# One division per head, a new order of units, and fewer first splits on VectorE in a hybrid encoder layer

## The chip, the cores and the metric

The kernel runs on one core of a Trainium2 chip. The metric is device microseconds of one execution, the median of several runs. TensorE (PE) does matrix products into PSUM, with its weight loads (PEld) beside them; VectorE (DVE) and ScalarE (ACT) do elementwise work on SBUF and PSUM; GpSimd (POOL) does elementwise work on SBUF; all transfers are issued from SyncE's queue (SP). TensorE's clock has two levels, 1.2 and 2.4 GHz; the profile gives the granted clock of a stretch as a share of the full one.

## The reference, cut to what matters

One layer over 2048 rows of 1024 columns, all in float32:

```python
h = rms_norm(x, norm_g)
proj = h @ w_in                       # 14 parts: a_q a_k a_v a_z m_q m_k m_v m_o m_z m_i m_f c_a c_b c_z
# A: band attention of 4 heads of 64 columns, 64-row chunks, 8 chunks back; gate silu(a_z)
# B: mLSTM of 4 heads of 128 columns:
num = s @ v + inter_w * (C @ q)       # s = (q k^T) * decay matrix
den = sum(s) + inter_w * (n . q)
h_ = num / max(|den|, exp(-m_t))
hm = rms_norm(sigmoid(m_o) * h_) * ml_out_g * silu(m_z)
# C: GLU of c_a, c_b; causal depthwise convolution of 31 taps; LayerNorm; silu; gate silu(c_z)
x = x + concat(A, B, C) @ w_out
```

## The kernel before, in words

The 2048 rows are worked off in four quarters (NQ) of 512, each of four blocks (NB) of 128. The work of a quarter is a list of *units*, each one projection: kv, qg (attention's q and the mLSTM gates, 264 columns), v and o (mLSTM) have rows on the partitions and go block by block (`tm`, lines 490 to 509); cb/ca (GLU), mk/mq/z (mLSTM k, q and gate of each head), az/cz (gates) and out0 to out7 (128 output columns each) have columns on the partitions and all 512 rows at once (`cm`, line 511). Each product is three passes: x and weights are each split into a rounded fp32r part and the rest, so one 128x512 result takes 3x8 = 24 matmuls.

The order of the units is written out by hand: FIRST for the first quarter, LATER + TAIL (lines 43 to 45) for the others. A quarter's eight outputs are the first units of the next list, mixed into it, and those of the last quarter stand alone at the end. Everything else (norms, attention, the mLSTM heads, convolutions) is written as generators, *chains*, that a planner in Python steps while it writes out the units' matmuls: it keeps a clock for every engine, with costs for each operation (lines 262 to 270), and puts a chain's next instructions into the program when their inputs should be ready by that clock. The order on each engine is fixed by that; on the chip only semaphores hold.

Weights come in pieces of 512 (qg: 528) columns through a ring of WB = 10 buffers. The first time, a piece is loaded raw (256 KB, four slots "W"), then split: a rounding copy and a subtraction. For the first eight pieces (kv's) the copies alternate between ACT and DVE and the subtractions between DVE and POOL; after that it is ACT and POOL (lines 450 and 451). The split piece is written to memory (512 KB) and later quarters load it from there. The first x is loaded in row blocks, its squares summed half on ACT and half on DVE (lines 556 to 561), the root taken on POOL, and then scaled and transposed on TensorE (`x_block`). x of later quarters arrives in transposed pieces k = 0 to 7 (`x_next`); only the first cb0 waits for them piece by piece (`xks`), and the outputs for the pieces of mT, the mixed result.

An mLSTM head (`head_chain`, line 963) multiplies, for each block, decayed scores and state into one PSUM tile, `ph`, of 129 columns: 128 numerators and, from a column of ones in vt, the denominator. DVE then updates the state `cst`, makes the reciprocal `rd` of the stabilised denominator in three [128x1] operations, and multiplies numerator, `rd` and the output gate `og` into `og` (lines 1019 to 1027). ACT sums the squares of each block. At the head's end POOL takes the root, ACT scales four blocks, TensorE transposes them (`pto`), and with the gate z they become a piece of mT. The 31-tap convolution runs as 60 DVE operations a quarter, `taps`, which the planner strews into DVE's free time; LayerNorm (`ln_chain`) is started behind mq3 and waits for the last tap. The last output unit is finished by one addition of 128x512 and one transfer.

Of the kernel before, what the change touches and what calls it, by code (L numbers as in the profile page):

```python
# [63 lines left out]
def kernel(ctx: ExitStack, tc: tile.TileContext, x, xT, wp, wq, norm_g, qg, kg, bias, far,  # L64
# [46 lines left out]
    def f(ap):  # L111
        return ap.bitcast(F32)
# [133 lines left out]
    class Engine:  # L246
# [3 lines left out]
        def __getattr__(self, name):  # L250
            fn = getattr(self.eng, name)

            def call(*a, **k):
# [174 lines left out]
    def feeder():  # L428
        while st["next"] < len(seq):
# [57 lines left out]

    PASS = ((0, 0), (0, 1), (1, 0))

    def tm(xt, u, b):  # L490
# [3 lines left out]
        step_ = 2 if gated else 1  # L494
        j0 = st["used"]
# [3 lines left out]
        for k in range(KT):  # L499
            w = piece((st["used"] if b == NB - 1 else j0 + k // step_))  # L500
            w = w[:, :, (k % step_) * n:(k % step_ + 1) * n] if gated else w
            need(xt[:, :, k, c])
# [8 lines left out]
    def cm(xt, u, ks=None):  # L511

        next_unit(u)
        ps = ps_new(u)
        i = 0
# [21 lines left out]
    def x_first(xt):  # L537
# [3 lines left out]
        big = io.tile([P, 2, D], F32, name="xbig", tag="og", bufs=1, cut=D)  # L541
# [8 lines left out]
        for b in range(NB):  # L550
# [4 lines left out]
            dump = ps_s.tile([P, D], F32, name="pdump", tag="s")  # L555
            A.activation(out=dump[:, 0:512], in_=t[:, 0:512], func=AF.Square, scale=1.0 / 32,
# [34 lines left out]
    def x_stat(q, rs, heads):  # L591
# [5 lines left out]
        big = io.tile([P, 2, D], F32, name="xbig", tag="og", bufs=1, cut=D)  # L597
# [243 lines left out]
    def gates(q, gt, FR, dd, cols, dec):  # L841
# [26 lines left out]
        R2_ = yield from take("R2", 256)  # L868
# [42 lines left out]
        shut(pt_)  # L911
        R2 = R2_[0:NR, :].rearrange("p (a b) -> p a b", a=2)
# [21 lines left out]
    def do_o(q, xt):  # L934
        next_unit("o")
        og = io.tile([P, NB, 512], F32, name="og", tag="og", bufs=1, cut=P)
        for b in range(NB):
            ps = tm(xt, "o", b)
            A.activation(out=og[:, b, :], in_=ps, func=AF.Tanh, scale=0.5)
            ps_done(ps)  # L940
            spawn(plus_one(og[:, b, :]))
        return og
# [20 lines left out]
    def head_chain(q, h, hb, vt, gc, cols, dec, FR, before):  # L963
# [43 lines left out]
        hs = slice(h * P, (h + 1) * P)  # L1007
        for b in range(NB):
# [25 lines left out]
        yield (rs,)  # L1034
        for b in range(NB):
            A.activation(out=og[:, b, hs], in_=og[:, b, hs], func=AF.Copy, scale=rs[:, b:b + 1])
# [3 lines left out]
        yield (og[:, :, hs],)  # L1040
        yield from bank_wait()
        pt, pt_ = bank("pto")
        for b in range(NB):
            tp(pt[:, b, :], og[:, b, hs])
# [18 lines left out]
    def do_conv(q, xt, j, ks=None):  # L1063
        pb = cm(xt, f"cb{j}", ks)
# [259 lines left out]
```

## Time and profile before

| | |
|---|---|
| median of 3 runs | 1214.1 us (1213.89 to 1214.77) |
| profiled execution | 1211.88 us, its span 1210.1 us, mean granted clock 0.993 |
| TensorE | 1172.0 us busy, 97% of the span |
| VectorE | 794.8 us, 66% |
| ScalarE | 432.7 us, 36% |
| GpSimd | 248.7 us, 21% |
| transfers | 240.25 MB, 199 GB/s on average |

The busy time of TensorE is modelled from pipelined matmuls; where it is busy throughout, the time of a group of 24 matmuls says how fast it goes. Idle time of an engine that is not the bottleneck costs nothing, so the shares are to be read stretch by stretch: the first quarter ends at about 282 us, and the last eight outputs begin at about 1161 us.

### The profile page before, as it was taken

To read this page: it belongs to the slowest core of one execution; us is meant where nothing else is said; L and a number is where in the kernel's file an instruction comes from. 1 tells how busy PE (TensorE), PEld (TensorE's weight loads), DVE (VectorE), ACT (ScalarE), POOL (GpSimd) and SP (SyncE) were. 2 spreads that over 40 slices of the span, in tenths; PEclk is the share of its full clock that TensorE was granted. 3 is DMA by queue.
4 is the path that set the end of the run, shared out by engine and by line. 5 is a ranking of instruction groups with operands and counts; after the bars stand their busy time and mean duration, and the time that the engine had idled before them with its cause. 6 is when DMAs were issued, how large, how long until landed. Compare 5 with 4: busy or idle time off the path is not lost.

```text
span 1210.1 us, 17636 instructions
## 1 busy us (share of the span) xinstructions
PE 1172.0 (97%) x6308; PEld 968.1 (80%) x6308; DVE 794.8 (66%) x1845; ACT 432.7 (36%) x984; POOL 248.7 (21%) x325
## 2 busy tenths in 40 slices
PE   6998998999999999999999999999999999999998
PEld 5776777777778888888888888888887988888886
DVE  6287888985568576775556766677447666677631
ACT  4454634443324441333232443233412344123310
POOL 5572545550232010111021100001002200011100
PEclk9998999998999999999999999999999999999999
DMA  9574848756774335654856351764684506375472
GB/s 356 167 302 158 305 153 300 263 209 205 270 260 143 114 132 199 238 173 155 298 197 232 123 175 53 278 200 143 213 292 160 205 27 213 131 251 164 157 230 101
DMA packets 95408, 240.25 MB, mean 199 GB/s; under 512 B 11288, under 2 KB 28248, under 8 KB 95320
## 3 DMA queue, kind: packets, MB, share of 16 engines
q1 hardware_dynamic: 95320, 239.11, 57.0%
q8 instruction: 50, 0.82, 0.3%
q14 instruction: 38, 0.31, 0.1%
HBM read 186.52 MB, written 52.56 MB: 198 GB/s over the span
## 4 chain that ended last, share of the span: by engine, by line
PE 83%; DVE 6%; DMA 4%; POOL 3%; issue 3%; ACT 1%; SPq 0%; POOLq 0%; ACTq 0%; DVEq 0%
PE pmm_out L311 13%; PE pmm_v L311 7%; PE pmm_z L311 7%; PE pmm_mk L311 7%; PE pmm_mq L311 6%; PE pmm_kv L311 6%; PE pmm_o L311 6%; PE pmm_cz L311 4%; PE pp L311 3%; PE pmm_qg L311 3%; PE po L311 3%; PE pmm_ca L311 3%; PE pss L311 3%; PE pmm_az L311 3%; PE ptp L316 3%
## 5 line engine op out<-in xcount | busy, mean ns | idle before, releaser
L254 DVE SCALAR_TENSOR_TENSOR cvu<-cvu,cvw_t 128x512 f32<-128x512 f32 x240 | 193.3, 806 | 10.9 <-ACT cvu L254 7.1
L311 PE MATMUL pmm_out<-mT,w 128*128 128x512 f32 x768 | 189.5, 398 | 2.8 <-DVE xr L254 1.7
L311 PEld LDWEIGHTS pmm_out<-mT,w 128*128 128x128 f32 x768 | 141.8, 188 | 34.7 <-DVE mT L254 2.5
L254 POOL TENSOR_TENSOR w<-rw,w 128x512 fp32r<-128x512 f32 (+1 forms) x80 | 114.3, 1443 | 175.6 <-ACT w L254 158.4
L311 PE MATMUL pmm_v<-w,xT 128*128 128x512 f32 x384 | 115.2, 417 | 1.2 <-POOL w L254 1.2
L311 PE MATMUL pmm_mk<-xT,w 128*128 128x512 f32 x384 | 106.2, 406 | 0.0
L311 PE MATMUL pmm_z<-xT,w 128*128 128x512 f32 x384 | 101.0, 409 | 0.0
L311 PE MATMUL pmm_mq<-xT,w 128*128 128x512 f32 x384 | 96.2, 397 | 0.0
L311 PE MATMUL pmm_o<-w,xT 128*128 128x512 f32 x384 | 95.4, 399 | 0.0
L311 PE MATMUL pmm_kv<-w,xT 128*128 128x512 f32 x384 | 94.2, 400 | 0.0
L311 PEld LDWEIGHTS pmm_kv<-w,xT 128*128 128x128 f32 x384 | 72.0, 190 | 16.0
L254 DVE SCALAR_TENSOR_TENSOR macc<-mraw,mcw_t,macc 128x512 f32<-128x512 f32 x96 | 79.4, 827 | 7.5 <-ACT macc L254 5.1
L311 PEld LDWEIGHTS pmm_z<-xT,w 128*128 128x128 f32 x384 | 72.4, 194 | 14.9
L311 PEld LDWEIGHTS pmm_o<-w,xT 128*128 128x128 f32 x384 | 71.0, 188 | 16.1 <-issue 0.9
L311 PEld LDWEIGHTS pmm_mq<-xT,w 128*128 128x128 f32 x384 | 71.0, 188 | 15.1 <-issue 0.5
L311 PEld LDWEIGHTS pmm_v<-w,xT 128*128 128x128 f32 x384 | 68.3, 191 | 15.0 <-POOL w L254 2.8
L311 PEld LDWEIGHTS pmm_mk<-xT,w 128*128 128x128 f32 x384 | 69.1, 189 | 13.2 <-issue 1.0
L254 POOL COPY mch<-mraw 128x3 f32<-128x3 f32 x32 | 11.0, 342 | 277.3 <-ACT mraw L254 276.9
L254 ACT CAST w<-rw 128x512 fp32r<-128x512 f32 (+1 forms) x80 | 49.1, 618 | 22.8 <-DMA rw<-in_wp 7.0
L254 ACT COPY pT<-ptp 128x384 f32<-128x384 f32 (+2 forms) x64 | 29.3, 459 | 77.7 <-PE ptp L316 77.6
L254 DVE TENSOR_TENSOR xr<-pmm_out,xr 128x512 f32<-128x512 f32 x32 | 22.0, 688 | 45.5 <-PE pmm_out L311 43.0
L311 PE MATMUL pmm_az<-xT,w 128*128 128x512 f32 x192 | 49.7, 401 | 0.0
(231 smaller groups left out, 1996.7 us busy)
## 6 DMA issues: line engine op xcount, KB each, us to landing
w<-wk SPq DMA_DIRECT2D x240, 512.0 KB, 4.4
wk<-w SPq DMA_DIRECT2D x80, 512.0 KB, 5.6
rw<-in_wp SPq DMA_DIRECT2D x80, 256.0 KB, 4.3
xr<-in_xT SPq DMA_DIRECT2D x32, 256.0 KB, 5.3
out<-xr SPq DMA_DIRECT2D x32, 256.0 KB, 5.3
xbig<-in_x SPq DMA_DIRECT2D x14, 512.0 KB, 6.9
w<-wk SPq DMA_DIRECT2D x12, 528.0 KB, 7.6
xk<-in_xT SPq DMA_DIRECT2D x24, 256.0 KB, 5.7
```

What stands on the lines that cost most here:

```text
L254: i = tc.keep_in_program_order(fn(*a, **k))
L311: tc.keep_in_program_order(PE.matmul(out_, lhsT=lhsT, rhs=rhs, start=start, stop=stop))
L316: tc.keep_in_program_order(PE.transpose(out=out_, in_=in_, identity=(ident_r if rnd else ident)[0:n, 0:n]))
```

## The change

- **Denominators.** `og` gets a 129th column a head, set to 1. The product from PSUM is taken 129 wide into it, so the denominator lands beside the gated numerators, undivided. After the fourth block `divide` makes the reciprocals of all four at once, ACT sums the squares with the reciprocal as scale, and the reciprocal is multiplied into the root before the head is scaled.
- **Order.** New lists FIRST, LATER and TAIL. `tm` too now waits for x piece by piece, by a table `filled`, since kv becomes the first unit that reads a later quarter's x.
- **First splits.** Of the first eight pieces DVE keeps the copy of piece 1 and the subtractions of pieces 0 and 3. The squares of the first x's blocks 1 to 3 are summed on ACT alone.
- **Last output.** The last unit is computed in two halves of 256 columns, each with its own addition and transfer.
- **Planner.** Other costs for POOL; the buffer R2 of the gates is taken later and from another set of slots.

```diff
-FIRST = ['kv', 'cb0', 'ca0', 'cb1', 'ca1', 'qg', 'v', 'mk0', 'mq0', 'o', 'mk1', 'mq1', 'az0', 'z0', 'mk2', 'mq2', 'az1', 'z1', 'mk3', 'mq3', 'cz0', 'cz1', 'z2', 'z3']
-LATER = ['out0', 'out1', 'out2', 'out3', 'cb0', 'ca0', 'kv', 'out4', 'cb1', 'ca1', 'qg', 'out5', 'v', 'mk0', 'mq0', 'o', 'out6', 'mk1', 'mq1', 'out7']
-TAIL = ['mk2', 'mq2', 'z0', 'mk3', 'mq3', 'z1', 'az0', 'az1', 'z2', 'cz0', 'cz1', 'z3']
+FIRST = ['kv', 'cb0', 'ca0', 'qg', 'cb1', 'ca1', 'v', 'mk0', 'mq0', 'o', 'mk1', 'mq1', 'az0', 'z0', 'mk2', 'mq2', 'cz0', 'mk3', 'mq3', 'az1', 'cz1', 'z1', 'z2', 'z3']
+LATER = ['out0', 'out1', 'out2', 'out3', 'kv', 'cb0', 'ca0', 'cb1', 'ca1', 'qg', 'v', 'out4', 'out5', 'out6', 'mk0', 'mq0', 'out7', 'o', 'mk1', 'mq1']
+TAIL = ['mk2', 'mq2', 'z0', 'cz0', 'mk3', 'mq3', 'az0', 'z1', 'z2', 'az1', 'cz1', 'z3']
...
                 elif k.get("op") == ALU.pow:
-                    d = 1.0
+                    d = 0.55 + 0.15 * n
                 else:
-                    d = 0.25 + (0.0021 * n if two else 0.0)
+                    d = 0.35 + (0.0019 * n if two else 0.0)
...
-                (V.tensor_copy if j < 8 and j % 2 else A.copy)(out=w[:, 0], in_=raw)
-                (V if j < 8 and j % 2 == 0 else G).tensor_tensor(out=w[:, 1], in0=raw, in1=f(w[:, 0]),
+                (V.tensor_copy if j in (1,) else A.copy)(out=w[:, 0], in_=raw)
+                (V if j in (0, 3) else G).tensor_tensor(out=w[:, 1], in0=raw, in1=f(w[:, 0]),
...
+    def halves(xt, u):
+        next_unit(u)
+        for c0 in (0, 256):
+            ps = ps_new(u)
+            i = 0
+            for k in range(KT):
+                w = piece(st["used"] + k // 4).rearrange("p a (k c) -> p a k c", k=4)
+                for s_, m_ in PASS:
+                    mm(ps[:, 0:256], w[:, s_, k % 4, :], xt[:, m_, k, c0:c0 + 256], i == 0, i == 3 * KT - 1)
...
+            yield c0, ps
...
+            if b >= 1:
+                A.activation(out=dump, in_=t, func=AF.Square, scale=1.0 / 32, accum_out=ss[:, 2 * b:2 * b + 1])
...
-        og = io.tile([P, NB, 512], F32, name="og", tag="og", bufs=1, cut=P)
+        og = io.tile([P, NB, 4, 129], F32, name="og", tag="og", bufs=1, cut=129)
+        G.memset(og.rearrange("p b h c -> p (b h) c")[:, :, 128:129], 1.0)
...
+        def divide(b0, b1):
+            dn, em = og[:, b0:b1, h, 128], cols[:, 2, h, b0:b1]
+            r_ = rd[:, b0:b1]
+            V.scalar_tensor_tensor(out=r_, in0=dn, scalar=-1.0, in1=em, op0=ALU.mult, op1=ALU.max)
+            V.tensor_tensor(out=r_, in0=dn, in1=r_, op=ALU.max)
+            V.reciprocal(out=r_, in_=r_)
+            yield (rd,)
+            for b in range(b0, b1):
+                A.activation(out=kw[:, b, :], in_=og[:, b, h, 0:128], func=AF.Square, scale=rd[:, b:b + 1],
+                             accum_out=ss[:, b:b + 1])
...
-            rd = sm.tile([P, 1], F32, name="rd", tag="rd")
-            em = cols[:, 2, h, b:b + 1]
-            V.tensor_scalar(out=rd, in0=ph[:, 128:129], scalar1=-1.0, scalar2=em, op0=ALU.mult, op1=ALU.max)
-            V.scalar_tensor_tensor(out=rd, in0=ph[:, 128:129], scalar=em, in1=rd, op0=ALU.max, op1=ALU.max)
-            V.reciprocal(out=rd, in_=rd)
-            hm = og[:, b, hs]
-            V.scalar_tensor_tensor(out=hm, in0=ph[:, 0:128], scalar=rd, in1=hm, op0=ALU.mult, op1=ALU.mult)
-            yield (hm,)
-            A.activation(out=kw[:, b, :], in_=hm, func=AF.Square, accum_out=ss[:, b:b + 1])
+            hm = og[:, b, h, :]
+            V.tensor_tensor(out=hm, in0=ph[:, 0:129], in1=hm, op=ALU.mult)
+            if b % 4 == 3:
+                yield from divide(b - 3, b + 1)
...
+        V.tensor_tensor(out=rs, in0=rs, in1=rd, op=ALU.mult)
...
-    for u in order_of(NQ):
+    for u in order_of(NQ)[:-1]:
         out_unit(int(u[3:]))
+    for c0, ps in halves(box["mt"][0], u_last := order_of(NQ)[-1]):
...
+        V.tensor_tensor(out=xr, in0=ps[:, 0:256], in1=xr, op=ALU.add)
+        ps_done(ps)
+        dma(out=out[i * P:(i + 1) * P, (NQ - 1) * TQ + c0:(NQ - 1) * TQ + c0 + 256], in_=xr)
```

## Rows read from the trace of the kernel before

**Rows 1.** Stretches: length, busy per engine, granted clock, transfers' share, GB/s.

```profile
core 0: us, PE busy (x) PEld busy (x) DVE busy (x) ACT busy (x) POOL busy (x), PEclk, DMA share, GB/s
81.60:100.00 18.40, 11.89 (x57) 8.00 (x56) 16.55 (x43) 9.04 (x23) 14.05 (x15) 0.93 0.59 200
100.00:146.00 46.00, 46.00 (x282) 35.24 (x280) 33.77 (x108) 27.89 (x72) 16.63 (x13) 0.95 0.61 218
...
170.00:200.00 30.00, 24.45 (x121) 20.46 (x121) 27.14 (x47) 13.80 (x32) 20.29 (x18) 0.94 0.98 350
200.00:240.00 40.00, 38.21 (x190) 31.38 (x189) 34.39 (x61) 17.04 (x38) 19.84 (x18) 1.00 0.70 237
...
268.00:288.00 20.00, 16.70 (x75) 13.01 (x73) 11.79 (x28) 10.27 (x24) 4.45 (x8) 0.83 0.34 119
...
700.00:800.00 100.00, 100.00 (x587) 81.98 (x587) 66.99 (x175) 31.49 (x72) 4.29 (x11) 1.00 0.53 184
```

**Rows 2.** Timeline of the start, TensorE: start us, us, engine, line, operation, tiles.

```profile
16.02 3.27 PE L311 MATMUL pmm_kv<-w,xT 128*128 128x512 f32 x7
```

**Rows 3.** The chain that ended last, in order of time: start, us, what.

```profile
602.39 5.55 PE pmm_cb L311 x24
...
654.33 9.08 PE pmm_qg L311 x75
...
893.86 5.55 PE pmm_cb L311 x24
...
928.97 5.60 PE pmm_out L311 x24
```

**Rows 4.** TensorE's waits: for whom, us in total, times, longest.

```profile
PE pS L311 <- DVE macc L254: 5.5, 2, 4.9
PE ptp L316 <- DVE pr L254: 3.3, 1, 3.3
```

**Rows 5.** Timeline between qg and v: POOL's splits, DVE's gate operations.

```profile
88.62 6.27 POOL L254 TENSOR_TENSOR w<-rw,w 128x512 fp32r<-128x512 f32 x5
...
92.46 4.47 DVE L254 SCALAR_TENSOR_TENSOR gpp<-gpp,gz 128x16 f32<-128x16 f32 x7
```

**Rows 6.** Tile rd: duration ns min/median/max, first and last start.

```profile
L254 DVE TENSOR_SCALAR rd<-pp,cols x64: 204/210/214, 175.8 to 1137.9; 128x1 f32<-128x1 f32 x64
L254 DVE SCALAR_TENSOR_TENSOR rd<-pp,cols,rd x64: 217/219/220, 176.1 to 1138.1; 128x1 f32<-128x1 f32 x64
L254 DVE RECIPROCAL rd<-rd x64: 162/164/167, 176.3 to 1138.4; 128x1 f32<-128x1 f32 x64
```

**Rows 7.** Tile og: ACT's squares, their sums, the scaling at a head's end.

```profile
L254 ACT ACTIVATE kw<-og x64: 301/311/314, 177.0 to 1139.0; 128x128 f32<-128x128 f32 x64
L254 ACT ACTIVATION_READ_ACCUMULATOR kw<-og x64: 185/187/203, 177.2 to 1139.2; 128x1 f32 x64
L254 ACT ACTIVATE og<-og,mrs x64: 384/388/405, 197.4 to 1142.1; 128x128 f32<-128x128 f32 x64
```

**Rows 8.** Tile w up to 110 us: the splits on POOL and DVE.

```profile
L254 POOL TENSOR_TENSOR w<-rw,w x26: 1262/1301/1782, 7.0 to 95.6; 128x512 fp32r<-128x512 f32 x22, 128x528 fp32r<-128x528 f32 x4
L254 DVE TENSOR_TENSOR w<-rw,w x4: 680/874/1099, 5.9 to 13.7; 128x512 fp32r<-128x512 f32 x4
L254 DVE CAST w<-rw x4: 410/420/1495, 6.5 to 14.3; 128x512 fp32r<-128x512 f32 x4
```

**Rows 9.** Timeline of the kernel's end: the last addition.

```profile
1205.97 0.69 DVE L254 TENSOR_TENSOR xr<-pmm_out,xr 128x512 f32<-128x512 f32 x1 [4.86 <-PE pmm_out L311]
```

**Rows 10.** Stretches of the last quarter, the convolution's tile cvu alone.

```profile
890.00:960.00 70.00, 0.00 (x0) 0.00 (x0) 29.08 (x39) 1.63 (x2) 0.63 (x3) 1.00 0.57 195
...
1040.00:1100.00 60.00, 0.00 (x0) 0.00 (x0) 14.31 (x20) 0.00 (x0) 0.00 (x0) 1.00 0.62 215
```

**Rows 11.** Timeline of the last quarter: last tap, first LayerNorm transpose, last head scaled.

```profile
1080.60 0.74 DVE L254 SCALAR_TENSOR_TENSOR cvu<-cvu,cvw_t 128x512 f32<-128x512 f32 x1
...
1115.70 0.38 PE L316 MATMUL ptl<-ident_r,cvu 128*128 128x128 f32 x2
...
1141.15 1.28 ACT L254 ACTIVATE og<-og,mrs 128x128 f32<-128x128 f32 x4 [0.25 <-POOL mrs L254]
```

More of the change, by code (lines that the diff above doesn't have):

```diff
@@ L486, in ps_done @@
         held[held.index(ps.tensor.name)] = None
+    filled = {}
     PASS = ((0, 0), (0, 1), (1, 0))
@@ L494, in tm @@
         step_ = 2 if gated else 1
+        ks = filled.get(xt.tensor.name)
         j0 = st["used"]
@@ L501, in tm @@
             w = w[:, :, (k % step_) * n:(k % step_ + 1) * n] if gated else w
+            if ks is not None:
+                wait_for(lambda: k in ks, f"{u} k{k}")
             need(xt[:, :, k, c])
@@ L509, in tm, with cm @@
         return ps
-    def cm(xt, u, ks=None):
+    def halves(xt, u):
[7 more added lines that the diff above has]
+                    mm(ps[:, 0:256], w[:, s_, k % 4, :], xt[:, m_, k, c0:c0 + 256], i == 0, i == 3 * KT - 1)
+                    i += 1
+                    tick()
+            yield c0, ps
+    def cm(xt, u):
         next_unit(u)
         ps = ps_new(u)
+        ks = filled.get(xt.tensor.name)
         i = 0
@@ L540, in x_first @@
         xs = [io.tile([P, D], F32, name="xs", tag="io", padded_shape=[P, 1056]) for _ in range(2)]
-        big = io.tile([P, 2, D], F32, name="xbig", tag="og", bufs=1, cut=D)
+        big = io.tile([P, 2, D], F32, name="xbig", tag="og", bufs=1, cut=D, padded_shape=[P, 2, D + 8])
         xs += [big[:, i, :] for i in range(2)]
@@ L596, in x_stat @@
         ss = sm.tile([P, NB], F32, name="xss4", tag="xss4", bufs=1)
-        big = io.tile([P, 2, D], F32, name="xbig", tag="og", bufs=1, cut=D)
+        big = io.tile([P, 2, D], F32, name="xbig", tag="og", bufs=1, cut=D, padded_shape=[P, 2, D + 8])
         for b in range(0, NB, 2):
@@ L867, in gates @@
         R_ = yield from take("R", 512)
-        R2_ = yield from take("R2", 256)
         yield from bank_wait()
@@ L911, in gates @@
         shut(pt_)
+        R2_ = yield from take("R2", 256, tag="B")
         R2 = R2_[0:NR, :].rearrange("p (a b) -> p a b", a=2)
@@ L935, in do_o @@
         next_unit("o")
-        og = io.tile([P, NB, 512], F32, name="og", tag="og", bufs=1, cut=P)
+        og = io.tile([P, NB, 4, 129], F32, name="og", tag="og", bufs=1, cut=129)
+        G.memset(og.rearrange("p b h c -> p (b h) c")[:, :, 128:129], 1.0)
         for b in range(NB):
             ps = tm(xt, "o", b)
-            A.activation(out=og[:, b, :], in_=ps, func=AF.Tanh, scale=0.5)
+            A.activation(out=og[:, b, :, 0:128], in_=ps.rearrange("p (h c) -> p h c", h=4), func=AF.Tanh, scale=0.5)
             ps_done(ps)
-            spawn(plus_one(og[:, b, :]))
+            spawn(plus_one(og[:, b, :, 0:128]))
         return og
@@ L1006, in head_chain @@
         mt = box["mT"]
-        hs = slice(h * P, (h + 1) * P)
+        rd = sm.tile([P, NB], F32, name="rd", tag="rd")
+        def divide(b0, b1):
[8 more added lines that the diff above has]
+                             accum_out=ss[:, b:b + 1])
         for b in range(NB):
@@ L1034, in head_chain @@
         yield (rs,)
+        V.tensor_tensor(out=rs, in0=rs, in1=rd, op=ALU.mult)
+        yield (rs,)
         for b in range(NB):
-            A.activation(out=og[:, b, hs], in_=og[:, b, hs], func=AF.Copy, scale=rs[:, b:b + 1])
+            A.activation(out=og[:, b, h, 0:128], in_=og[:, b, h, 0:128], func=AF.Copy, scale=rs[:, b:b + 1])
         hb["want"] = True
@@ L1039, in head_chain @@
             yield 0.3
-        yield (og[:, :, hs],)
+        yield (og[:, :, h, 0:128],)
         yield from bank_wait()
@@ L1043, in head_chain @@
         for b in range(NB):
-            tp(pt[:, b, :], og[:, b, hs])
+            tp(pt[:, b, :], og[:, b, h, 0:128])
         gz = box.pop(("z", h))
@@ L1060, in do_head, with do_conv @@
         return hb
-    def do_conv(q, xt, j, ks=None):
-        pb = cm(xt, f"cb{j}", ks)
+    def do_conv(q, xt, j):
+        pb = cm(xt, f"cb{j}")
         t = grab("cvt", 512)
@@ L1173, in out_unit @@
             fetch_x(i + 1)
[L1174 removed]
+        ps = cm(box["mt"][0], f"out{i}")
         step(spawn(finish(i, ps, box["mt"][1])))
@@ L1227 @@
                 if h == 0:
-                    box["mT"] = (xtile(f"mT_{q}"), q, set())
+                    mt_ = xtile(f"mT_{q}")
+                    box["mT"] = (mt_, q, filled.setdefault(mt_.tensor.name, set()))
                 heads.append(do_head(q, xt, h, vt, gc, cols_, dec, FR, heads[-1] if heads else None))
@@ L1247 @@
             xt = xtile(f"xT_{q + 1}")
-            xks = set()
+            xks = filled.setdefault(xt.tensor.name, set())
             spawn(x_next(q + 1, xt, nrs, lnc, xks))
-    for u in order_of(NQ):
+    for u in order_of(NQ)[:-1]:
         out_unit(int(u[3:]))
+    xr = None
+    for c0, ps in halves(box["mt"][0], u_last := order_of(NQ)[-1]):
+        i = int(u_last[3:])
+        wait_for(lambda: ("xr", NQ - 1, i) in box)
+        xr = box["xr", NQ - 1, i][:, c0:c0 + 256]
+        V.tensor_tensor(out=xr, in0=ps[:, 0:256], in1=xr, op=ALU.add)
+        ps_done(ps)
+        dma(out=out[i * P:(i + 1) * P, (NQ - 1) * TQ + c0:(NQ - 1) * TQ + c0 + 256], in_=xr)
     wait_for(lambda: not chains, "end")
```

9 lines of the change are left out of this document (6 added, 3 removed).

## The prediction

> **What bounds the kernel now.** I read the page's busy shares, then its 40 slices, then stretches of equal work, then TensorE's waits, then the tiles that the change touches. The page gives a TensorE that is 97% busy, so the reader has to ask where the other 3%, and the slices with a granted clock under full, are. The stretches answer: from 700 to 800 us TensorE has no idle time and a clock of 1.00 with DVE at 67%; the loss sits in the first quarter [rows 1]. Idle time is length minus busy; a stretch at clock c loses (1-c) of its length, since the two levels are 1.2 and 2.4 GHz. That gives 81.6 to 100: 6.5 idle, 1.3 clock; 100 to 146: 2.3 clock; 170 to 200: 5.5 idle, 1.8 clock; 200 to 240: 1.8 idle; 268 to 288: 3.3 idle, 3.4 clock. Sum 25.9 us, to which the 16.0 us before the first projection matmul come [rows 2]. A later quarter repeats itself to the tenth: cb0 begins at 602.39 and again at 893.86, 291.5 us apart [rows 3]; it is matmul work, and order can win little there. The waits name what is late in the first quarter: mLSTM's score matmuls wait 5.5 us for the causal convolution on DVE, the first transposes of attention 3.3 us for DVE's normalised row [rows 4]; DVE is busy 27.1 of 30 us and 34.4 of 40 us in the two mLSTM stretches.
>
> So the change can win at most some 26 us in the middle of the first quarter, 3 at its start, 2 at the end of the kernel; what it risks are three quarters of which each is full.
>
> **First order of units.** qg goes ahead of cb1 and ca1. Now v follows qg at once: v's first block wants eight new weight pieces within 24 matmuls of 0.231 us (a 24-matmul unit takes 5.55 us, [rows 3]), while attention and the gates only begin. POOL delivers five pieces in 6.27 us from 88.62, so 1.25 us each against the 0.69 that TensorE would take; at the same time seven tiny gate operations take 4.47 us on DVE [rows 5], and the rows of attention wait behind them. After the change two units, 11.1 us of matmuls with four pieces, stand between qg and v, and attention's first scores run inside them. At stake are 6.5+1.3+2.3 = 10.1 us. The pieces arrive no faster, so part of the wait for v stays. Bounds 0 and -10; I take the middle, -5.
>
> **Denominators.** Each of 64 blocks loses three [128x1] operations of 0.210, 0.219 and 0.164 us [rows 6], 2.37 us a head of four blocks; each of 16 heads gains three on [128x4] and one multiply for them. The nearest rows are the removed ones, so 0.8 us; the trace of before has no [128x4] form of them, and bounds from the same rows are 0.65 (four at 0.164) and 0.9 (four at 0.219). Net -1.6 us a head, -6.3 a quarter on DVE. The product from PSUM becomes 129 columns wide and keeps its cost. The squares move behind the division and carry a scale: the nearest ACTIVATE with one takes 0.388 us against 0.311, plus 0.187 for reading the sum [rows 7], so four of them stand as 2.3 us at the end of each head instead of one block's 0.5. The head's end then is about 1.8+0.2-0.6 = 1.4 us later, against some 0.6 us a block that its PSUM comes free earlier, 2.4 a head: even. Where DVE is nearly full, 170 to 240 us with 9.1 us at stake, two and a half heads return 4 us of DVE; I take -3.5, bounds 0 and -9. In later quarters TensorE is full and the DVE time is worth nothing by itself. Writing 1 into the extra column, the strided [128x4x128] forms of tanh and of the added 1: off the path, since DVE has a third of each later quarter free [rows 1]; if that cover went, 16 additions at twice today's cost would be 7 us of DVE.
>
> **End of the first quarter.** Between mq3 and the outputs now stand cz0, cz1, z2, z3; then az1, cz1, z1, z2, z3, one unit of 5.55 us more to cover LayerNorm and the last head, and less DVE work before it. 6.7 us at stake; taken -2, bounds +3 (conv 1's taps start behind qg, 96 times 0.121 us = 11.6 us later) and -6.
>
> **First splits.** DVE loses three casts (0.42 each, one took 1.50), two subtractions net (0.87) and three sums of squares (0.77 with the read): 5.3 us by medians. ACT gains three casts and the other halves of three squares, some 3 us; POOL gains two subtractions of 1.30 [rows 8]. DVE is what keeps block 0's transposed x until about 16 us [rows 2], so the first matmuls can start earlier; but POOL, which also does the roots for blocks 1 to 3, delivers six of the eight first pieces instead of four. Taken -1.5, bounds -3 and +3.
>
> The Trainium skill, GPSIMD Engine Reference, § 8 Key points, says that VectorE is structurally about twice as fast for elementwise work and that the two share SBUF interfaces, so a subtraction moved to GpSimd costs it more than VectorE gains. The trace has 1.5 times (1301 against 874 ns), and the sharing in casts that range from 410 to 1495 ns. By that rule this term would be +2.6 instead of -1.5, and the sum -5.9; it stands below as the third rival.
>
> **Last output in halves.** The last addition begins at 1205.97 and takes 0.69 [rows 9]; from its end to the end of the span (1210.1) pass 3.44 us. Half the columns: addition about 0.4, transfer between 3.41 and half of it. 48 matmuls of 256 columns in place of 24 of 512: qg's 264-column ones run at 9.08/75 = 0.121 us [rows 3], so 5.81 against 5.55, +0.26. Bounds +0.26 and -1.8; taken -0.3-0.45+0.26 = -0.5.
>
> **Later quarters.** kv goes ahead of both convolutions, and the outputs 4 to 6 behind v. kv as the first consumer asks for the next x piece by piece just as cb0 did, so that wait stays where it is. qg and v become neighbours as in the first order now, but weights then come ready from memory without POOL. The new costs of POOL in the planner move single instructions; I can't size that and put all of it here. Taken +2.5 for three quarters, bounds -3 and +12 (next but one paragraph).
>
> **Sum.** -5 -3.5 -2 -1.5 -0.5 +2.5 = -10.0. The profiled execution took 1211.9 us (span 1210.1 and 1.8 around it), so 1201.9; the runs' median, 1214.1, is 2.2 above it, so the prediction is 1204.
>
> **Rivals.** (1) *The convolution's taps come too late*, and the three later quarters pay: slower than before. cb0 and ca0 from 893.86 take 11.1 us, so kv lasts from 904.96 to the output at 928.97 [rows 3], and conv 0's taps will start 24 us later. In 890 to 960 some 37 taps ran [rows 10], 0.67 a us from 905 on, so 16 are missing by then; afterwards they go at 20 in 40 us up to the last one at 1080.60 [rows 10, 11], so the last would fall 33 us later, near 1114, where LayerNorm starts today (1115.70). For it: DVE's free third is also what attention needs. Against: qg is 7 us earlier than today, DVE gets 6 us back, and the outputs that LayerNorm feeds lie six units, 33 us, and their first 18 matmuls behind mq3, of which LayerNorm needs about 25 if it is as long as a head. It decides once the taps end over 12 us after mq3; the price I set is one uncovered unit, 6 us a quarter, 18 in all: 1204+18 = 1222. The last head has the same tail: from mq3's end (about the first LayerNorm transpose) to its scaled output at 1141.15 pass 25 us [rows 11], and five units of 5.55, 28 us, with attention's and the heads' own matmuls between them, still cover it.
> (2) *The first quarter is bound by the arrival of weights*: POOL, its slots and the transfers keep their pace, and the order only moves the waits. For it: the 1.25 us a piece. Against: the transfers' share is 0.59 in the stretch with the most idle time, and the longest waits name DVE [rows 1, 4]. Then only DVE's relief (-2), the tail and the later quarters' cost remain: about 1214.
> (3) *POOL bounds the start*: 1204+4 = 1208.
> (4) *Nearly all of it comes back*: 20 of the 25.9 us, the later quarters stay free: 1214.1-22.5 = about 1192. For it: idle time and slow clock stand in the same stretches, so what removes the one gives back the other.
>
> **How the numbers follow.** Forecast 0.48, rival 1 0.14, rival 2 0.13, rival 3 0.10, rival 4 0.15. What a measurement here can tell from no change is 0.2%, 2.4 us. Faster: 0.46 of the forecast, 0.15, 0.08 of rival 3, 0.03 of rival 2: 0.72. Slower: rival 1 and 0.02 of rival 2: 0.16. The rest, 0.12, is the same. The range reaches down to rival 4 and up to where half of rival 1 is in: 1191 to 1218; the forecast's own range is 1197 to 1210.
>
> **What would show it.** Right: idle time and slow clock between qg and the end of v fall by half; the score matmuls' 5.5 us wait for the convolution falls under 3; the first kv matmul stands before 16 us; from the last matmul to the end about 3.3 us; cb0 to cb0 stays within 1 us of 291.5. Wrong: a later quarter over 294 us, with TensorE waiting at the first output for LayerNorm; or v's wait for POOL grown by what left the DVE waits.

## The result and the profile after

The changed kernel takes 1195.0 us (median of 4 runs, 1192.4 to 1197.2); the kernel before took 1214.0 in the same rounds (1212.8 to 1214.8). The ratio is 0.9843, 95% interval 0.9822 to 0.9865: 1.6% faster, 19 us, of which 10 were forecast. 1195.0 lies inside the range and just outside the forecast's own range of 1197 to 1210. The profiled execution has a span of 1193.5 us, 16.6 less than before. The page's busy shares:

```profile
PE 1167.3 (98%) x6332; PEld 964.5 (81%) x6332; DVE 761.6 (64%) x1707; ACT 434.5 (36%) x987; POOL 242.5 (20%) x331
```

DVE lost 33.2 us of work (794.8 before). Where TensorE's time came from, the stretches tell (length, busy time of each engine with its instructions, granted clock, the transfers' share, GB/s), next to [rows 1]:

```profile
81.60:100.00 18.40, 17.18 (x103) 12.79 (x101) 15.10 (x45) 12.46 (x36) 10.11 (x11) 1.00 0.77 249
100.00:146.00 46.00, 46.00 (x262) 36.08 (x263) 36.39 (x84) 24.10 (x55) 19.70 (x17) 1.00 0.60 209
...
170.00:200.00 30.00, 25.93 (x113) 20.62 (x113) 27.04 (x37) 13.96 (x32) 15.73 (x14) 0.89 0.87 310
200.00:240.00 40.00, 38.16 (x194) 31.42 (x193) 36.09 (x62) 19.75 (x47) 21.73 (x21) 1.00 0.74 247
...
268.00:288.00 20.00, 20.00 (x96) 16.53 (x95) 10.90 (x17) 7.14 (x14) 0.00 (x0) 1.00 0.85 281
288.00:300.00 12.00, 9.89 (x39) 6.66 (x37) 6.39 (x10) 2.50 (x5) 0.00 (x0) 1.00 0.76 277
...
700.00:800.00 100.00, 100.00 (x557) 82.37 (x556) 73.12 (x154) 30.08 (x70) 7.99 (x17) 1.00 0.53 174
```

Counted as the prediction counted: 81.6 to 146 lost 10.1 us and loses 1.2; 268 to 288 lost 6.7 and loses nothing, but 288 to 300 now loses 2.1; 170 to 240 lost 9.1 and still loses 9.2 (4.1 idle, 3.3 clock, 1.8 idle). The windows are fixed in time and the changed kernel is up to 17 us ahead, so late ones don't hold the same work: from 240 to 330 us, over the end of the first quarter, the loss is 8.7 before and 4.6 after. TensorE's waits (for whom, us in total, times, longest) show what is left:

```profile
PE pxt L311 <- ACT dg L254: 8.5, 2, 6.7
PE pS L311 <- DVE macc L254: 2.9, 2, 1.8
PE pmm_mk L311 <- DVE az L254: 2.9, 1, 2.9
PE pmm_kv L311 <- ACT xT L254: 2.3, 3, 0.8
```

The score matmuls' wait for the causal convolution went from 5.5 to 2.9 us [rows 4], and attention's wait for its normalised row left the top of the list. (pxt are the transposes of the first x at the start; pmm_ before a name marks the matmuls of that unit.) The timeline (start, us, engine, operation) of the kernel's start, of the second quarter's first unit and of the end:

```profile
10.25 1.69 PE L311 MATMUL pmm_kv<-w,xT 128*128 128x512 f32 x5
...
44.45 2.94 PE L311 MATMUL pmm_cb<-xT,w 128*128 128x512 f32 x12
...
291.80 3.64 PE L311 MATMUL pmm_kv<-w,xT 128*128 128x512 f32 x15
296.12 1.23 PE L311 MATMUL pmm_kv<-w,xT 128*128 128x512 f32 x3 [0.68 <-ACT xT L254]
298.15 1.23 PE L311 MATMUL pmm_kv<-w,xT 128*128 128x512 f32 x3 [0.81 <-ACT xT L254]
...
1190.21 0.42 DVE L254 TENSOR_TENSOR xr<-pmm_out,xr 128x256 f32<-128x256 f32 x1 [2.43 <-PE pmm_out L311]
```

The first unit behind the fourth output marks a quarter's border. By TensorE's timeline it began at 308.9, 602.2 and 893.7 us before (the last two are the cb units that the chain of [rows 3] puts at 602.39 and 893.86), and begins at 291.8, 587.7 and 878.7 now. So the first quarter gave 17.1 us, the second took 2.5 back, the third gave 0.4 and the last, with its end, 1.6: together the 16.6 of the span. The prediction's sign, cb0 to cb0 within 1 us of 291.5, holds (290.6 and 291.0); from kv to kv the second quarter takes 295.9 us, for kv waits for x at its head.

### The profile page after: what moved, and what is told of

Read it like the earlier page. It is cut to its first block, busy times and chain, and to the rows that moved or that the text cites. A ratio compares the mean times of both kernels' runs of the same rounds, so it can differ in the third digit from the quotient of the medians.

```text
span 1193.5 us, 17535 instructions
## 1 busy us (share of the span) xinstructions
PE 1167.3 (98%) x6332; PEld 964.5 (81%) x6332; DVE 761.6 (64%) x1707; ACT 434.5 (36%) x987; POOL 242.5 (20%) x331
## 4 chain that ended last, share of the span: by engine, by line
PE 90%; DVE 6%; ACT 1%; DMA 1%; issue 1%; POOL 1%; SPq 0%; POOLq 0%; ACTq 0%
PE pmm_out L311 14%; PE pmm_v L311 8%; PE pmm_mq L311 7%; PE pmm_o L311 7%; PE pmm_mk L311 7%; PE pmm_z L311 7%; PE pmm_kv L311 6%; PE pmm_ca L311 4%; PE pp L311 4%; PE pmm_az L311 4%; PE pmm_qg L311 3%; PE pmm_cb L311 3%; PE pmm_cz L311 3%; PE po L311 3%; PE pss L311 3%; PE ptp L316 3%
## 5 line engine op out<-in xcount | busy, mean ns | idle before, releaser
L311 PE MATMUL pmm_out<-mT,w 128*128 128x512 f32 (+1 forms) x792 | 197.1, 394 | 0.5 <-DVE mT L254 0.5
L254 POOL TENSOR_TENSOR w<-rw,w 128x512 fp32r<-128x512 f32 (+1 forms) x82 | 117.6, 1448 | 132.8 <-ACT w L254 119.2
L311 PE MATMUL pmm_v<-w,xT 128*128 128x512 f32 x384 | 108.8, 408 | 0.0
L311 PE MATMUL pmm_kv<-w,xT 128*128 128x512 f32 x384 | 97.2, 406 | 2.3 <-ACT xT L254 2.3
L311 PE MATMUL pmm_o<-w,xT 128*128 128x512 f32 x384 | 90.0, 394 | 0.0
L311 PEld LDWEIGHTS pmm_z<-xT,w 128*128 128x128 f32 x384 | 69.4, 189 | 13.2
L254 DVE TENSOR_TENSOR xr<-pmm_out,xr 128x512 f32<-128x512 f32 (+1 forms) x33 | 22.2, 672 | 47.8 <-PE pmm_out L311 46.3
L254 ACT ACTIVATE pr<-pr,nm 128x640 f32<-128x640 f32 (+4 forms) x64 | 48.7, 762 | 3.8 <-DVE li L254 2.6
```

Source lines behind the costliest of these rows:

```text
L254: i = tc.keep_in_program_order(fn(*a, **k))
L311: tc.keep_in_program_order(PE.matmul(out_, lhsT=lhsT, rhs=rhs, start=start, stop=stop))
```

## The experiments

**What was to be told apart.** Theory: the parts of the change are not a sum. The new lists pack each quarter so that LayerNorm of the convolution branch is ready only just before the outputs need it; what pays for that is the VectorE time that the new division frees for the 60 taps of a quarter. First rival: the parts are independent, each worth its own term. Second rival: the old division costs by its latency, since each block's square goes into the tile that the next block reads, and not by VectorE's time (from one block's product to the next 4.1 us in the median of the later quarters, against 1.6; the expectation below says 3.2). Twelve kernels ran; each ratio is against the kernel before on the same chip. The first four share a chip; there the kernel before took 1210.5 us.

**Old first list.**

```
-FIRST = ['kv', 'cb0', 'ca0', 'qg', 'cb1', 'ca1', 'v', 'mk0', 'mq0', 'o', 'mk1', 'mq1', 'az0', 'z0', 'mk2', 'mq2', 'cz0', 'mk3', 'mq3', 'az1', 'cz1', 'z1', 'z2', 'z3']
+FIRST = ['kv', 'cb0', 'ca0', 'cb1', 'ca1', 'qg', 'v', 'mk0', 'mq0', 'o', 'mk1', 'mq1', 'az0', 'z0', 'mk2', 'mq2', 'az1', 'z1', 'mk3', 'mq3', 'cz0', 'cz1', 'z2', 'z3']
```

> The changed kernel (1195.0) with the old FIRST list alone. Theory: the order of the first quarter holds the gain, since the losses between qg and the end of v fell by 8.9 us and those before the outputs by 6; then this kernel takes 1205 to 1210, with the idle time back behind qg. Rival (POOL's new costs or the freed VectorE made the gain, whatever the order): under 1199.

Measured: 1200.4 us, ratio 0.9914 (0.9897 to 0.9931), in neither range: the list is worth some 5 us by the medians and 8.6 by the ratios (0.9914 against 0.9843, measured on two chips). All of it is gained in the first quarter: the borders stand 10.1, 7.5 and 7.5 us later than the changed kernel's.

**Old lists of the later quarters.**

```
-LATER = ['out0', 'out1', 'out2', 'out3', 'kv', 'cb0', 'ca0', 'cb1', 'ca1', 'qg', 'v', 'out4', 'out5', 'out6', 'mk0', 'mq0', 'out7', 'o', 'mk1', 'mq1']
-TAIL = ['mk2', 'mq2', 'z0', 'cz0', 'mk3', 'mq3', 'az0', 'z1', 'z2', 'az1', 'cz1', 'z3']
+LATER = ['out0', 'out1', 'out2', 'out3', 'cb0', 'ca0', 'kv', 'out4', 'cb1', 'ca1', 'qg', 'out5', 'v', 'mk0', 'mq0', 'o', 'out6', 'mk1', 'mq1', 'out7']
+TAIL = ['mk2', 'mq2', 'z0', 'mk3', 'mq3', 'z1', 'az0', 'az1', 'z2', 'cz0', 'cz1', 'z3']
```

> The changed kernel with the old LATER and TAIL. Theory: the new later lists bring nothing and cost the waits of kv for x at the start of the second quarter (2.3 us idle, about 2 us of slow clock), so 1191 to 1195. Rival (the later lists carry a part of the gain, because outputs 4 to 6 now cover attention): 1198 or more.

Measured: 1205.5 us, 0.9951 (0.9933 to 0.9968). The rival held: the new lists are worth 10 us by the medians, 13 by the ratios. Most of the loss (7.2 us between the second and third border) stands at the head of the second quarter, where cb0 waits for the last pieces of the new x: 4.95 us in one wait, and a granted clock of 0.89 from 300 to 330.

**Old division in each block.**

```
...
-            hm = og[:, b, h, :]
-            V.tensor_tensor(out=hm, in0=ph[:, 0:129], in1=hm, op=ALU.mult)
-            if b % 4 == 3:
-                yield from divide(b - 3, b + 1)
...
+            V.tensor_scalar(out=rd, in0=ph[:, 128:129], scalar1=-1.0, scalar2=em, op0=ALU.mult, op1=ALU.max)
+            V.scalar_tensor_tensor(out=rd, in0=ph[:, 128:129], scalar=em, in1=rd, op0=ALU.max, op1=ALU.max)
+            V.reciprocal(out=rd, in_=rd)
+            hm = og[:, b, h, 0:128]
+            V.scalar_tensor_tensor(out=hm, in0=ph[:, 0:128], scalar=rd, in1=hm, op0=ALU.mult, op1=ALU.mult)
+            yield (hm,)
+            A.activation(out=kw[:, b, :], in_=hm, func=AF.Square, accum_out=ss[:, b:b + 1])
...
```

> The changed kernel with the old division, three small operations and a square for each block. Theory: VectorE's relief counts little, for the two mLSTM stretches lose as much time after as before (9 us), so 1195 to 1198. Rival (28 us less of small operations is what let the first quarter close up): 1202 or more, with VectorE 25 to 30 us busier.

Measured: 1227.0 us, 1.0129 (1.0107 to 1.0151), slower than the kernel before: the rival held. More than half of the loss, 16.7 of 31.3 us of span, stands before the second border (308.5 against 291.8). After it the third quarter takes 296.9 us instead of 291.0 and the last, with its end, 7.5 more, and TensorE waits at each quarter's first output. Its timeline at the last one:

```profile
1159.05 0.38 PE L316 MATMUL ptl<-ident_r,cvu 128*128 128x128 f32 x2
...
1167.78 0.49 PE L316 MATMUL pty<-ident_r,cvu 128*128 128x128 f32 x3
1169.71 0.33 PE L316 MATMUL pty<-ident_r,cvu 128*128 128x128 f32 x1 [1.44 <-DVE cvu L254]
...
1173.63 1.22 PE L311 MATMUL pmm_out<-mT,w 128*128 128x512 f32 x2 [3.15 <-DVE cz L254]
```

LayerNorm's first transposes (ptl) come at 1159, 31.5 us after mq3's end at 1127.5, and the outputs wait for its second half (pty transposes back, cz is the gate). The rows of the tile cvu (count: shortest, median, longest ns, first to last start) in the last quarter, first of this kernel, then of the changed one, say why:

```profile
L254 DVE SCALAR_TENSOR_TENSOR cvu<-cvu,cvw_t x60: 740/750/754, 939.2 to 1158.0; 128x512 f32<-128x512 f32 x60
```

```profile
L254 DVE SCALAR_TENSOR_TENSOR cvu<-cvu,cvw_t x60: 721/747/754, 915.4 to 1099.9; 128x512 f32<-128x512 f32 x60
```

A tap costs the same 0.75 us, but the 60 are spread over 219 us instead of 184. In the changed kernel the last ends 4.3 us before mq3 does (1105.0), here 31 us behind it.

**Old planner costs.** POOL's two cost lines as before.

```
-                    d = 0.55 + 0.15 * n
+                    d = 1.0
...
-                    d = 0.35 + (0.0019 * n if two else 0.0)
+                    d = 0.25 + (0.0021 * n if two else 0.0)
```

> The changed kernel with the planner's old costs for GpSimd. Theory: they shift single instructions, 1194 to 1198. Rival (with the old costs the planner puts TensorE's instructions before their inputs are ready, and most of the gain goes): 1203 or more.

Measured: 1195.3 us, 0.9864 (0.9844 to 0.9884), as expected; the costs decide nothing that can be seen here (the interval overlaps the changed kernel's). The other slots of the buffer R2 were not taken back in any run of the changed kernel.

**Denominators alone.** The kernel before, with the new division and nothing else. These four kernels share a chip, on which the kernel before took 1211.9 us.

> The kernel before with the denominator change alone (old lists of units, old splits, old costs, one last addition). Theory: with the old per-block division the convolution's taps end late and LayerNorm with them, and the old lists lived with that because there conv's first unit comes before kv and the outputs are spread; so the denominators alone give a few us in the first quarter's mLSTM stretch, 1203 to 1209 us. Rival (the blocks' latency costs under the old lists as much as under the new): below 1198. Second rival (VectorE time off the path is worth nothing): 1212 to 1215.

Measured: 1213.1 us, 1.0002 (0.9986 to 1.0019): nothing, as the second rival had it. Its borders say where the gain went. The second quarter begins at 299.8, 9.1 us earlier than before, and the third at 602.23, where it began before. Two stretches in which it gained and the one behind them, then the timeline there:

```profile
170.00:200.00 30.00, 27.05 (x132) 21.56 (x130) 28.68 (x41) 15.17 (x35) 22.44 (x19) 1.00 0.85 308
...
268.00:288.00 20.00, 19.68 (x97) 16.02 (x96) 11.35 (x17) 11.54 (x29) 2.70 (x3) 1.00 0.67 222
...
300.00:400.00 100.00, 92.08 (x482) 74.96 (x481) 63.30 (x153) 32.57 (x71) 23.85 (x28) 0.97 0.52 188
```

```profile
299.80 4.57 PE L311 MATMUL pmm_cb<-xT,w 128*128 128x512 f32 x18
...
311.33 1.95 PE L311 MATMUL pmm_cb<-xT,w 128*128 128x512 f32 x3 [4.92 <-ACT xT L254]
```

cb0 needs the eighth piece of x after 5 us, and it comes at 311: its load was issued at 301.9 and took 8.0 us. In the kernel before the same piece was cast at 309.1, so it is the arrival of x that the old later lists wait for when the first quarter ends early. In the changed kernel the last piece is cast at 299.5. So the old lists gave the whole gain back, and the new ones bring most of it home; why that load is issued so late under the old ones was not taken apart.

**First list alone.** The kernel before with the new FIRST.

> The kernel before with the first quarter's new list alone. Theory (the new lists need the new denominators: with the old ones the first quarter's taps end late and its outputs wait): the 9 us of the stretch at 81.6 to 146 us are mostly given back at the end of the first quarter, 1209 to 1217 us. Rival (the first quarter's list and the denominators are independent): 1203 to 1206 us, as taking the list back out of the changed kernel cost 5.4 us there.

Measured: 1214.7 us, 1.0025 (1.0007 to 1.0044). Theory. It gains 8.4 us between 81.6 and 146, as the changed kernel does, and loses it from 240 us on, where the first outputs wait for the activations (4.9 us) and LayerNorm's first transposes for the taps (3.4 us):

```profile
240.00:268.00 28.00, 23.56 (x131) 19.89 (x130) 24.62 (x58) 11.81 (x34) 13.16 (x12) 0.99 0.52 187
268.00:288.00 20.00, 13.62 (x63) 10.33 (x61) 8.74 (x18) 7.19 (x16) 2.88 (x8) 0.84 0.36 118
288.00:300.00 12.00, 11.35 (x37) 9.06 (x38) 6.76 (x11) 2.48 (x4) 0.00 (x0) 0.72 0.61 198
```

**The old work, without the old chain.** The changed kernel, with the three small operations of the old division done in each block as well, into a tile (r1) that nothing else reads.

```
...
+            V.tensor_scalar(out=r1, in0=ph[:, 128:129], scalar1=-1.0, scalar2=em, op0=ALU.mult, op1=ALU.max)
+            V.scalar_tensor_tensor(out=r1, in0=ph[:, 128:129], scalar=em, in1=r1, op0=ALU.max, op1=ALU.max)
+            V.reciprocal(out=r1, in_=r1)
             V.tensor_tensor(out=hm, in0=ph[:, 0:129], in1=hm, op=ALU.mult)
```

> The changed kernel with the three [128x1] operations on PSUM of the old division put back in each block, ahead of the product; their result is used by nothing. The VectorE work per block is that of the old loop, but no block waits for the square of the one before. Theory (the loss of the old division is VectorE time, which the taps then lack): 1215 us or more, with the last tap near 1140 us or later, as in the run with the old division (1227 us). Rival (the loss is the chain in each block, product, square into the tile that the next block reads, at 3.2 us a block against 1.6): 1195 to 1201 us.

Measured: 1230.3 us, 1.0148 (1.0121 to 1.0174). Theory: no block waits for a square here, the products follow each other 2.3 us apart in the median of the later quarters, and the loss is as large. The last tap starts at 1161.7. The page's busy shares, and the taps of the last quarter:

```profile
PE 1178.7 (96%) x6332; PEld 973.5 (79%) x6332; DVE 791.0 (64%) x1899; ACT 434.0 (35%) x987; POOL 238.8 (19%) x331
...
L254 DVE SCALAR_TENSOR_TENSOR cvu<-cvu,cvw_t x60: 742/750/755, 941.0 to 1161.7; 128x512 f32<-128x512 f32 x60
```

29.4 us more work on an engine that is 64% busy in both kernels made the span 34.6 us longer, 8.0 to 9.1 us in each later quarter and 8.5 in the first. In the first it isn't the taps: they end earlier than in the changed kernel (the last one at 231.1 us against 242.9), and the score matmuls wait 8.6 us for the causal convolution on VectorE instead of 2.9.

**Old division, taps let out more freely.**

```
-TAP = 1.0
+TAP = 0.5
...
-        while taps and free["V"] <= clk["t"] + 0.3 and clk["t"] - clk["tap"] >= TAP:
+        while taps and free["V"] <= clk["t"] + 1.5 and clk["t"] - clk["tap"] >= TAP:
...
```

> The changed kernel with the old per-block division, and with the taps let out more freely: one every 0.5 us at least of the planner's time instead of 1.0, and with VectorE planned up to 1.5 us ahead instead of 0.3. Theory (VectorE has the time, it is 64 to 67% busy, and the planner's rule for letting taps out leaves it idle): most of the 32 us go, 1198 to 1207 us. Rival (VectorE itself is short in the stretch between the conv units and the end of a quarter): 1218 us or more.

Measured: 1215.5 us, 1.0029 (1.0013 to 1.0046), between the two and nearer the rival: by the medians, 11.5 of the 32 us came back. The taps of the last quarter now run from 932.5 to 1065.1, in 133 us:

```profile
L254 DVE SCALAR_TENSOR_TENSOR cvu<-cvu,cvw_t x60: 741/752/754, 932.5 to 1065.1; 128x512 f32<-128x512 f32 x60
```

So VectorE had the time in the later quarters, and it was the planner's rule (one tap in 1.0 us at most, and only where VectorE is planned to be free within 0.3 us; the two were loosened together) that held the taps back behind the small operations. The later quarters take 295.6 and 293.1 us, 0.3 less and 2.1 more than the changed kernel's, although the products of a head are as far apart as in the kernel with the old division (4.1 us in the median): with that the second rival falls for the later quarters. What is left is mostly the first quarter (second border at 307.2 instead of 291.8), so there the rival's shortage of VectorE may hold. The looser rule was not tried with the new division. In the first quarter, from 81.6 to 100 TensorE is busy 13.2 of 18.4 us again at a clock of 0.76.

**Later lists alone.** The kernel before with the new LATER and TAIL and the waits piece by piece that they need. The next three kernels share a chip with the kernel before at 1212.8 us.

> The kernel before with the lists of the later quarters alone (LATER and TAIL, with the waits piece by piece that they need); old first list, old division, old splits. Theory (the new lists hold only while VectorE has the time that the new denominators free): each later quarter pays 5 to 8 us at its outputs, as in the runs with the old division, 1222 to 1235 us. Rival (the lists are harmless by themselves, and only the new first list and the old division clash): 1203 to 1212 us.

Measured: 1226.5 us, 1.0113 (1.0089 to 1.0138). Theory: the lists are a loss without the new division; the last tap starts at 1149.8, and the outputs wait 6.0 us for cz.

The lists and the division, then, as ratios to the kernel before. The four with two or three parts (0.9951, 0.9914, 1.0129, 0.9843) also hold the small edits (splits, costs, halves, R2), and the rows come from several chips; each ratio is good to about 0.2%.

| lists | old division | new division |
|---|---|---|
| both old | 1 | 1.0002 |
| new FIRST | 1.0025 | 0.9951 |
| new LATER and TAIL | 1.0113 | 0.9914 |
| both new | 1.0129 | 0.9843 |

The division is worth 0 with the old lists, 0.7% with the first, 2.0% with the later ones, 2.9% with both; the 0.7 and 2.0 include the small edits.

**Old first splits and squares.** The changed kernel with both back on VectorE as before.

```
-                (V.tensor_copy if j in (1,) else A.copy)(out=w[:, 0], in_=raw)
+                (V.tensor_copy if j < 8 and j % 2 else A.copy)(out=w[:, 0], in_=raw)
-                (V if j in (0, 3) else G).tensor_tensor(out=w[:, 1], in0=raw, in1=f(w[:, 0]),
+                (V if j < 8 and j % 2 == 0 else G).tensor_tensor(out=w[:, 1], in0=raw, in1=f(w[:, 0]),
...
-            if b >= 1:
+            if b >= 99:
```

> The changed kernel with the first weight splits and the squares of the first x blocks put back on VectorE (old splits, old squares). Theory (the start was bound by VectorE's share of the splits and squares, first kv matmul at 10.3 against 16.0 us, the end of kv 1.9 us earlier): 1 to 3 us slower than the changed kernel. Rival (POOL's subtractions or the arrival of the weights bound the start, or kv's end is absorbed by the waits behind it): within 0.5 us of the changed kernel.

Measured: 1194.8 us, 0.9848 (0.9825 to 0.9871): nearer the rival, though an interval of 0.23% to either side, 2.8 us, doesn't rule out the theory's 1 to 3. The trace is clearer. The first cb0 begins at 46.8 us instead of 44.5 and the second quarter at 293.6 instead of 291.8, but there kv waits for x less (1.6 us against 2.3), and the third begins at 586.9 against 587.7. What the start gains is given back to the arrival of x.

**Fifth output ahead of kv.** In all later quarters, then in the second alone.

```
-LATER = ['out0', 'out1', 'out2', 'out3', 'kv', 'cb0', 'ca0', 'cb1', 'ca1', 'qg', 'v', 'out4', 'out5', 'out6', 'mk0', 'mq0', 'out7', 'o', 'mk1', 'mq1']
+LATER = ['out0', 'out1', 'out2', 'out3', 'out4', 'kv', 'cb0', 'ca0', 'cb1', 'ca1', 'qg', 'v', 'out5', 'out6', 'mk0', 'mq0', 'out7', 'o', 'mk1', 'mq1']
```

> The changed kernel with the fifth output unit moved from behind v to ahead of kv in the later quarters, so that kv begins 5.7 us later against the x pieces it waits for. Theory (the waits of kv for x after 288 us, 2.3 us and a lower clock around them, are all that the second quarter still loses there, and nothing in the later quarters hangs on kv's place): 2 to 3 us faster than the changed kernel, a ratio of 0.9820 +- 0.0015. Rival (the conv units come 5.7 us later and the taps end later by as much, so LayerNorm is late at the outputs): each quarter pays, 1200 us or more.

Measured: 1194.0 us, 0.9843 (0.9821 to 0.9866): in neither range, and no difference from the changed kernel. Kv to kv, the second quarter fell from 295.9 to 291.3 us, but the third grew from 291.1 to 292.2, and outputs now wait 1.7 us for the activations before the third border and 0.8 before the fourth. Hence the last kernel, where LATER2 is that list:

```
-    return [f"out{i}" for i in range(8)] if q == NQ else LATER + TAIL if q else FIRST
+    return [f"out{i}" for i in range(8)] if q == NQ else LATER2 + TAIL if q == 1 else LATER + TAIL if q else FIRST
```

> The changed kernel with the fifth output unit ahead of kv in the second quarter alone; the third and fourth quarters keep the changed kernel's list. Theory (with the unit moved in all three later quarters, the second quarter gained about 4 us, 295.9 to 291.3 us from kv to kv, and the third and fourth lost 1 us each where outputs waited for the activations' last pieces): the gain stays and the losses go, 2.5 to 4.5 us faster than the changed kernel, a ratio of 0.9805 to 0.9825. Rival (what the second quarter gains is given back behind it whatever the later list): a ratio of 0.9840 to 0.9850, as with the unit moved everywhere.

Measured: 1191.6 us (1190.6 to 1193.1) against 1212.3 for the kernel before there, 0.9835 (0.9817 to 0.9853). Kv's three starts:

```profile
297.23 11.07 PE L312 MATMUL pmm_kv<-w,xT 128*128 128x512 f32 x47
...
582.87 11.07 PE L312 MATMUL pmm_kv<-w,xT 128*128 128x512 f32 x47
...
873.98 11.06 PE L312 MATMUL pmm_kv<-w,xT 128*128 128x512 f32 x47
```

The second quarter takes 285.6 us (one output fewer of 5.7 in it, so 291.3), the third 291.1, and the span is 1188.8 us against 1193.5. The trace agrees with the theory, but the ratio lies between the two ranges, nearer the rival's, and its interval reaches into both: by the ratios it is 1 us faster than the changed kernel, by the medians of two chips 3.4, and not shown to be faster.

## Why the prediction was right, and where not

The direction and the place, the first quarter, were right; the size was 19 us instead of 10. Of the 6.6 us by which the span missed the sum, 5.1 lie before the second border (17.1 us gained, 12 forecast in four terms) and 1.5 behind it. That the range held the result is partly luck: its lower end was set by rival 4, whose reason didn't come true.

What the sum had wrong is that its terms add up. The second border shows it: 308.9 us in the kernel before, 310.1 with the new first list alone, 299.8 with the denominators alone, and 291.8 with everything; with everything but the list it stands at 301.9, with everything but the denominators at 308.5. So the list is worth -1 us without the denominators and 10 with them, and the denominators 9 without the list and 17 with it. The steps:

- **First order, -5.** The stretch it names returned 8.9 of the 10.1 us at stake, so "part of the wait for v stays" was too careful: with two units between qg and v, TensorE waited no longer for POOL there. But the term isn't the list's own. Alone it came to 1.0025, since the end of the quarter takes it back; in the changed kernel it is worth 5 to 9 us. Bounds that were drawn from the stretch alone couldn't show that.
- **Denominators, -3.5.** The work per head was sized well. These are the changed kernel's rows of rd and og (columns as in [rows 6]):

```profile
L254 DVE SCALAR_TENSOR_TENSOR rd<-og,cols x16: 161/162/166, 171.7 to 1124.4; 128x4 f32<-128x4 f32 x16
L254 DVE TENSOR_TENSOR rd<-og,rd x16: 161/161/164, 171.9 to 1124.5; 128x4 f32<-128x4 f32 x16
L254 DVE RECIPROCAL rd<-rd x16: 177/178/179, 172.1 to 1124.7; 128x4 f32<-128x4 f32 x16
L254 DVE TENSOR_TENSOR mrs<-mrs,rd x16: 146/153/1259, 181.7 to 1130.9; 128x4 f32<-128x4 f32 x16
L254 DVE TENSOR_TENSOR og<-pp,og x64: 278/285/288, 166.2 to 1124.0; 128x129 f32<-128x129 f32 x64
```

  They add 0.65 us a head for the 2.37 removed, and the denominators alone took 24.4 us off VectorE, 25 forecast. "Keeps its cost" was a small miss: the product without a scalar takes 0.285 instead of 0.351 us, which saves 0.26 a head more. The Trainium skill (VectorE: DVE Perf Modes, section on the TRN2 errata) says that operations with a source in SBUF pay a fixed extra cost per instruction, which weighs the less the larger the operand; the rows agree, 0.16 to 0.18 us for four columns from SBUF against 0.16 to 0.22 for one, two of the three of these from PSUM [rows 6]. The step that failed is "in later quarters ... the DVE time is worth nothing by itself". That holds for the old lists (a later quarter of the kernel with the denominators alone takes 292.1 us, 291.5 before) and is wrong for the new ones: there 7 to 9 us of VectorE work a quarter cost 6 to 9 us of time in the third (296.9 and 300.1 against 291.0), as long as the planner's rule for the taps stands. And the place of the -3.5 was only half right: 170 to 240 us lost 9.1 before and 9.2 after, but 12.6 with the old division under the new lists, 19.6 with the old work put back, and 7.1 with the denominators alone. So the relief does pay there, and the rest of the change takes as much back; at 268 to 288 the denominators alone return 6.4 of the 6.7 us.
- **End of the first quarter, -2.** From 240 to 330 us 4.1 came back: 6.7 returned at 268 to 288, 2.0 lost on balance right behind, where kv waits for x, and 0.6 ahead. It isn't the order's own: with the new list alone 240 to 300 us lose 11 us more than before, and with the denominators alone 268 to 288 lose 0.3.
- **First splits, -1.5.** The mechanism was right, first kv matmul at 10.25 instead of 16.02 us and the end of kv 1.9 earlier (splits and squares were not taken apart); at the end nothing of it can be seen, and what it would meet (the pieces of x at the next border) was not asked. The third rival, POOL bounding the start, did not come: with the subtractions moved to POOL the start is earlier. The prediction's ratio of 1.5 between the engines came from a median of disturbed subtractions; the shortest ones of [rows 8], 0.680 and 1.262 us, give 1.9. That agrees with the rule of the Trainium skill (GPSIMD Engine Reference, § 8 Key points), but the +2.6 that the prediction drew from it does not come at the start, where the trace has the end of kv earlier.
- **Last output in halves, -0.5.** The addition takes 0.42 instead of 0.69 us, and from its end to the end of the span pass 2.9 us instead of 3.4: -0.8 with both, against -0.75 forecast before the matmuls' +0.26. No run took it alone.
- **Later quarters, +2.5.** The borders give +0.5 with the end, 1.5 under the two terms' +2.0. As a cost of the lists, though, it was the wrong question: without them 10 to 13 us of the gain are lost.
- **Rival 1** was the right mechanism. Its price, 6 us a quarter, is what the kernel with the old division pays (296.9 against 291.0), and its condition, taps ending over 12 us after mq3, is met there (31 us) and not in the changed kernel, where they end before mq3. The prediction named the relief that DVE gets as one of three reasons against it; the runs show that under the planner's rule it decides.
- **Rival 4** gave the time best, 1192, though for another reason than "idle time and clock go together": 9 us in the mLSTM stretches were not recovered, and lists and division paid together.

## What to carry to other kernels

An engine's busy share doesn't say what its time is worth: ask which chain of small steps (here the taps) must be through before the next stage, and how much room lies between the two. Parts of a change that move work and parts that free time for it are to be priced together, as a table with each alone and each left out; a gain at the end of one stage counts only if the next stage's inputs are there earlier as well. The Trainium skill (Perfetto Trace Analysis, Identifying the Most-Contended Engine) advises to optimize first the engine with the highest occupancy, and to judge TensorE by other measures than its busy share; here some 30 us of work on an engine that is 64% busy moved the time by 35, more than either list of units did, and only TensorE's waits showed it. And before work is taken off an engine, ask who decides when its work starts: with two constants of the planner changed, the old division cost a later quarter 2.1 us at most.

## What the runs showed of the hardware

- Granted clock and idle time did not always go together: 170 to 200 us has less idle time than before (4.1 against 5.5 us) and a lower clock (0.89 against 0.94), so the stretch gained nothing.
- VectorE's operations with all their inputs in SBUF took longer where they began during one of POOL's weight subtractions. A [128x4] multiply on VectorE that takes 0.153 us took 1.26 once, at 181.68 us, while a subtraction of POOL's (1.75 us from 181.17) was under way. Of the changed kernel's 336 taps and steps of the causal convolution (macc), 31 began during such a subtraction: 29 of them ended 0.55 us after its end and took up to 1.84 us, and two came in its last 0.06 us. None of the others took over 0.76, nor did the 14 that began just before a subtraction. Operations with an input in PSUM kept their time: the product og<-pp,og took 0.28 to 0.29 us all four times. An example (start, us, engine), three steps that take 0.75 us elsewhere beside four subtractions:

```profile
184.87 6.53 POOL L254 TENSOR_TENSOR w<-rw,w 128x512 fp32r<-128x512 f32 x4 [1.22 <-ACT w L254]
...
185.10 5.17 DVE L254 SCALAR_TENSOR_TENSOR macc<-mraw,mcw_t,macc 128x512 f32<-128x512 f32 x3
```

  The 29 are longer by 23.6 us in all, 14.0 of them between 146 and 290 us, where the first quarter still splits weights on POOL and VectorE is nearly full. This is read from the times in the trace; no run moved POOL's subtractions away.
